# A Mamba-2 plus Conformer layer: first phase with more tiles in finer blocks, and the gate pairs of branch A kept in DRAM

## The chip, the core and the metric

The kernel runs on one core of a Trainium2 chip. A core has five engines with queues of their own: TensorE (PE, with its weight loads shown apart as PEld), VectorE (DVE), ScalarE (ACT), GpSimd (POOL) and SyncE (SP), which here only issues DMAs. Each engine carries out its instructions in the order in which the program was laid down and waits on semaphores. The metric is the time of one launch in device microseconds, the median of three runs.

## The reference

One layer over 256 latent tokens x and 256 context tokens, d = 2048, everything fp32.

```
shift, scale, gate (two sets) = split(silu(c) @ w_mod + b_mod, 6)      # the same for c_ctx
hx = rmsnorm(x) * (1 + scale) + shift                                  # 2048 channels
z, xbc, dt, glu, gates = split(hx @ w_in)                              # 4096, 6144, 128, 4096, 4096
xbc = silu(conv5(xbc)); x, B, C = split(xbc)                           # 4096, 8 x 128, 8 x 128
y = scan forwards and backwards over (x, B, C, softplus(dt)), 8 groups of 8 heads, chunks of 128;
    the latent scan starts from the context's last state
y_a = rmsnorm((y + d_skip * x) * silu(z)) @ w_proj_a
cf  = silu(layernorm(conv31(u * sigmoid(v)))) ; y_b = cf @ w_proj_b    # u, v = glu
x  += gate1 * ((sigmoid(g_a) * y_a + sigmoid(g_b) * y_b) @ w_out)
x  += gate2 * swiglu(modulate(rmsnorm(x)))
out = rmsnorm(x)
```

Context tokens only feed the scan's starting state, so of the projection they need x, B and dt (and not z, C, glu or the gates).

## The kernel before

Channels lie on the partitions and tokens on the free axis: 512 columns are 256 latent tokens followed by 256 context tokens. Each weight tile is loaded as fp32 (the name w, six buffers, 512 KB each, issued on SP), split into a rounded part wh by an ACT cast (line 113) and the rest wl by a DVE subtraction (line 114), and both are given a high scheduling priority. hx is kept as such a pair too. A unit is one weight tile of some k rows of 128 and 256 output columns. A "wide" 128-column tile gives results for all 512 tokens with three matmuls of 512 columns per k (lines 143, 144, 146); a "narrow" one serves latent tokens alone with one matmul of 512 columns and one of 256 (lines 151, 153). x, B and dt are wide; C, z, glu and the gates are narrow, and of a narrow tile the two halves of the accumulator are added by fold (lines 157 to 161: an ACT copy and a DVE addition for each of two tiles). Accumulators come from a PSUM pool named acc with four buffers, so two pairs of tiles.

**Phase one.** hx is not known at the start: its shift and scale come from w_mod (33.5 MB for these two). So the 16 k are cut into blocks, BLOCKS = (1, 1, 2, 2, 2, 4, 4) at line 32. While block q is computed, w_mod for block q+1 is fetched and multiplied by mod_units (matmuls in line 370, a small one in line 377, transposes of x in line 389). Of each block, six units are computed: dt; two pairs of x tiles each for groups 0 and 1; B and C of group 0. Each has its own accumulator, and DVE adds the block's part to a sum in SBUF (line 469; the sum of dt is dt_raw). In the last block the sum goes to a scratch tile, and conv (line 236) follows on it: an ACT pass, four DVE taps (line 246) and a Silu on ACT (line 249). After dt of the last block, dt_chain computes softplus, the cumulative sums and the weights wx.

**The scan stages.** Eight stages, one for each group: a generator ssd(stage - 1) is advanced beside a list of tasks, each of which computes one pair of tiles over all 16 k in four units. In stage 1 these are bcpair(1) (B and C of group 1), xpair(2, 0) and xpair(2, 1) (the x tiles of group 2); later stages add zpair (z, the output gate). The scan begins with transposes of B and x into PSUM, yfm (ACT, line 578), a copy btok (line 580), the weighing of x by wx (DVE, line 566) and the first matmuls with it (lines 585 and 586). gpair computes a pair of tiles of the first branch's gates g_a: one in stage 7 and four in stage 8, held in xc buffers.

**After the scan.** A stage that normalizes the Conformer branch (layernorm) is advanced beside the other eleven gate pairs, three of g_a and eight of g_b. Then come the two projections, w_out, and the FFN. A background stream computes the remaining four vectors of w_mod on DVE; a hook called once per unit advances it by 102 steps in 226 calls. At the end of each half vector it has a reduction over the partitions (matmuls in line 499, an ACT copy, transposes in line 504).

The order of instructions is made by a scheduler from the program text, with the high-priority parts moved forward by up to 450 instructions.

## Time and profile before

| | us |
|---|---|
| median of 3 runs | 2410.69 (2408.48 to 2411.11) |
| the profiled execution | 2409.69 |
| its span (first to last instruction) | 2407.9 |
| PE busy / weight loads | 2346.0 / 1976.3 |
| DVE / ACT / POOL busy | 1639.7 / 1266.5 / 131.2 |
| data moved | 509.41 MB, mean 212 GB/s |

A span is what the profiler saw from the first instruction to the last; 1.8 us of the profiled execution lie outside it. PEclk is the TensorE clock granted in a stretch, as a share of the full one. "Idle before" in a timeline's brackets is the time that the engine waited ahead of the instruction, and the arrow names what ended the wait. A tile's name stands without its number.

### The profile page before, as it was taken

To read this page: it belongs to the slowest core of one execution; us is meant where nothing else is said; L and a number is where in the kernel's file an instruction comes from. 1 tells how busy PE (TensorE), PEld (TensorE's weight loads), DVE (VectorE), ACT (ScalarE), POOL (GpSimd) and SP (SyncE) were. 2 spreads that over 40 slices of the span, in tenths; PEclk is the share of its full clock that TensorE was granted. 3 is DMA by queue.
4 is the path that set the end of the run, shared out by engine and by line. 5 is a ranking of instruction groups with operands and counts; after the bars stand their busy time and mean duration, and the time that the engine had idled before them with its cause. 6 is when DMAs were issued, how large, how long until landed. Compare 5 with 4: busy or idle time off the path is not lost.

```text
span 2407.9 us, 35235 instructions
## 1 busy us (share of the span) xinstructions
PE 2346.0 (97%) x13400; PEld 1976.3 (82%) x13400; DVE 1639.7 (68%) x2134; ACT 1266.5 (53%) x1980; POOL 131.2 (5%) x165
## 2 busy tenths in 40 slices
PE   6899999999999999999999999999999999999998
PEld 3668788888888788888888888888888888888888
DVE  4559867676676876888978676777666666655554
ACT  4335866656566675554575444446444444444443
POOL 1000000100000000010300000010000000000000
PEclk9999999999999999999999999999999999999999
DMA  9984445545455566888789887896777677766663
GB/s 280 289 280 139 134 135 153 160 125 162 136 148 155 163 199 192 266 264 282 246 267 295 261 282 251 276 288 190 219 231 223 210 230 225 222 193 193 192 192 114
DMA packets 468457, 509.41 MB, mean 212 GB/s; under 512 B 18147, under 2 KB 438194, under 8 KB 467776
## 3 DMA queue, kind: packets, MB, share of 16 engines
q1 hardware_dynamic: 461936, 488.74, 66.4%
q0 software_dynamic: 5792, 17.35, 2.2%
q8 instruction: 105, 1.72, 0.3%
q10 hardware_dynamic: 560, 1.08, 0.1%
q14 instruction: 64, 0.52, 0.1%
HBM read 496.35 MB, written 10.75 MB: 211 GB/s over the span
## 4 chain that ended last, share of the span: by engine, by line
PE 84%; DMA 7%; issue 4%; DVE 4%; ACT 2%; POOL 0%; SPq 0%; DVEq 0%; ACTq 0%; POOLq 0%
PE acc L151 38%; PE acc L153 20%; PE acc L143 6%; PE acc L144 6%; PE acc L146 6%; DMA w<-in_w_mod_dram 4%; PE acc L155 2%; DVE wl L114 2%; PE ss L667 1%; DMA cs<-cs_d 1%; PE ss L637 1%; PE tp L558 1%; PE ss L370 1%; DMA w<-in_w_in_dram 1%; DMA yst<-yg_d 1%
## 5 line engine op out<-in xcount | busy, mean ns | idle before, releaser
L114 DVE TENSOR_TENSOR wl<-w,wh 128x1024 fp32r<-128x1024 f32 (+3 forms) x702 | 847.2, 1211 | 486.0 <-ACT wh L113 484.8
L113 ACT CAST wh<-w 128x1024 fp32r<-128x1024 f32 (+3 forms) x702 | 717.0, 1023 | 703.8 <-PE acc L151 459.4
L151 PE MATMUL acc<-hx,wh 128*128 128x512 f32 x1556 | 433.0, 397 | 0.0
L151 PE MATMUL acc<-h,wh 128*128 128x512 f32 x1320 | 366.9, 397 | 4.7 <-DVE h L985 2.4
L151 PEld LDWEIGHTS acc<-hx,wh 128*128 128x128 f32 x1556 | 271.6, 189 | 40.9 <-issue 2.6
L153 PEld LDWEIGHTS acc<-hx,wl 128*128 128x128 f32 x1664 | 254.8, 188 | 35.6
L143 PE MATMUL acc<-hx,wh 128*128 128x512 f32 x656 | 265.7, 406 | 4.1 <-ACT wh L113 3.0
L153 PE MATMUL acc<-hx,wl 128*128 128x256 f32 x1664 | 264.9, 281 | 0.0
L151 PEld LDWEIGHTS acc<-h,wh 128*128 128x128 f32 x1320 | 231.5, 190 | 38.9 <-issue 4.5
L144 PE MATMUL acc<-hx,wh 128*128 128x512 f32 x656 | 259.2, 396 | 0.0
L153 PEld LDWEIGHTS acc<-h,wl 128*128 128x128 f32 x1408 | 215.9, 189 | 30.1
L493 DVE SCALAR_TENSOR_TENSOR mac<-w,silc,mac 128x1024 f32<-128x1024 f32 x120 | 154.7, 1289 | 120.2 <-DMA w<-in_w_mod_dram 119.8
L153 PE MATMUL acc<-h,wl 128*128 128x256 f32 x1408 | 223.7, 281 | 0.0
L146 PE MATMUL acc<-hx,wl 128*128 128x512 f32 x656 | 184.2, 394 | 0.0
L151 PE MATMUL acc<-hid,wh 128*128 128x512 f32 x602 | 166.3, 396 | 0.0
L143 PEld LDWEIGHTS acc<-hx,wh 128*128 128x128 f32 x656 | 123.8, 189 | 39.8 <-ACT wh L113 7.9
L146 PEld LDWEIGHTS acc<-hx,wl 128*128 128x128 f32 x656 | 123.9, 189 | 27.8 <-DVE wl L114 0.8
L144 PEld LDWEIGHTS acc<-hx,wh 128*128 128x128 f32 x656 | 124.2, 189 | 25.7 <-issue 1.6
L151 PE MATMUL acc<-yg,wh 128*128 128x512 f32 x496 | 136.6, 395 | 0.0
L151 PEld LDWEIGHTS acc<-hid,wh 128*128 128x128 f32 x602 | 103.6, 189 | 13.8
L153 PEld LDWEIGHTS acc<-hid,wl 128*128 128x128 f32 x616 | 94.4, 189 | 13.1
L618 ACT ACTIVATE cs<-cs,ncs 128x128 f32<-128x128 f32 x256 | 81.6, 390 | 32.4 <-DMA cs<-cs_d 30.6
(350 smaller groups left out, 2743.3 us busy)
## 6 DMA issues: line engine op xcount, KB each, us to landing
w<-in_w_in_dram SPq DMA_DIRECT2D x248, 512.0 KB, 4.3
w<-in_w_mod_dram SPq DMA_DIRECT2D x192, 512.0 KB, 4.9
w<-in_w_ffn_gate_dram SPq DMA_DIRECT2D x88, 512.0 KB, 4.5
w<-in_w_ffn_up_dram SPq DMA_DIRECT2D x88, 512.0 KB, 4.6
w<-in_w_ffn_down_dram SPq DMA_DIRECT2D x88, 512.0 KB, 3.5
w<-in_w_proj_a_dram SPq DMA_DIRECT2D x64, 512.0 KB, 5.2
w<-in_w_in_dram SPq DMA_DIRECT2D x74, 256.0 KB, 3.9
cs<-cs_d SPq DMA_DIRECT2D x32, 512.0 KB, 5.6
```

Of the source, the lines that this page charges most:

```text
L113: A.copy(out=hi[:, :n], in_=t[:, :n])
L114: V.tensor_tensor(out=lo[:, :n], in0=t[:, :n], in1=hi[:, :n].bitcast(F32), op=ALU.subtract)
L143: E.matmul(o, wj(hi, k), act(kofs + k)[:, 0, :ncol], start=kofs + k == kbeg, stop=False)
L144: E.matmul(o, wj(hi, k), act(kofs + k)[:, 1, :ncol], start=False, stop=False)
L146: E.matmul(o, wj(lo, k), act(kofs + k)[:, 0, :ncol], start=False, stop=last and k == nk - 1)
L151: E.matmul(o2, wj(hi, k), act(kofs + k)[:, :, :T], start=kofs + k == kbeg, stop=False)
L153: E.matmul(o[:, :T], wj(lo, k), act(kofs + k)[:, 0, :T], start=False, stop=last and not hold)
L155: E.matmul(o2, wj(hi, nk - 1), act(kofs + nk - 1)[:, :, :T], start=False, stop=True)
L370: E.matmul(b[32 * j:32 * j + 32, :fb], sil[:, rr, :], wt[:, r, :], start=rr < 4, stop=rr >= KD - 4)
L493: V.scalar_tensor_tensor(out=ac, in0=wt, scalar=silc[:, k - 1:k], in1=ac, op0=ALU.mult, op1=ALU.add)
L558: E.transpose(out=b[:, i * P:(i + 1) * P], in_=v, identity=ident)
L618: A.activation(out=t4[:, r, j], in_=t4[:, r, j], func=AF.Identity, bias=ncs[:, cc, r * 64 + hs + j:r * 64 + hs + j + 1])
```

## The change

Phase one has the blocks (1, 1, 2, 2, 2, 2, 2, 4) and takes eight units in each: B and C of group 1 and the first pair of x tiles of group 2 are added. Stage 1 of the scan therefore has neither bcpair(1) nor xpair(2, 0); it gets three gate pairs, and xpair(2, 1) after them. Stage 7 has one gate pair as before, stage 8 four, so all eight of g_a are done by the end of the scan. Each gate pair is folded into a tile named sz (one buffer) and stored by a POOL DMA to a DRAM scratch, eg_d; after the scan eight POOL DMAs load them back into ga, and sigmoid and the multiplication with the branch's 1/rms follow at the start of the normalizing stage, which now has only the eight pairs of g_b, and hands out layernorm's steps by a table. The xc pool has ten buffers instead of nine; sta and y share buffers of other tags. The hook is called 224 times rather than 236, at the same 102 in 226 (the reduction at its end has lines 503 and 508 after the change).

```diff
--- before.py
+++ after.py
@@ -29,7 +29,7 @@
 UK = 4
 UB = UK * 256
 NW32, NWH, NWL = 6, 4, 4
-BLOCKS = (1, 1, 2, 2, 2, 4, 4)
+BLOCKS = (1, 1, 2, 2, 2, 2, 2, 4)
 HP = 450
 NSTEP = 15
 
@@ -80,6 +80,7 @@
 
     xT_d = dpool.tile([P, KD, T], F32, name="xT_d")
     x1_d = dpool.tile([P, KD, T], F32, name="x1_d")
+    eg_d = dpool.tile([P, KD, T], F32, name="eg_d")
     yg_d = dpool.tile([P, 32, T], F32, name="yg_d")
     cs_d = dpool.tile([2, P, P], F32, name="cs_d")
     ec_d = dpool.tile([2, P, P], F32, name="ec_d")
@@ -225,7 +226,7 @@
     pa1 = pas.enter_context(pool("pa1", "right"))
 
     def xct():
-        return pa1.tile([P, 512], F32, tag="xc", name="xc", bufs=9)
+        return pa1.tile([P, 512], F32, tag="xc", name="xc", bufs=10)
 
     def bt():
         return pa1.tile([P, 512], F32, tag="Bt", name="Bt", bufs=2)
@@ -319,9 +320,9 @@
         V.tensor_copy(out=sel, in_=ident[:, 0:2])
         for j in range(1, 4):
             V.tensor_tensor(out=sel, in0=sel, in1=ident[:, 32 * j:32 * j + 2], op=ALU.add)
-        sta = p0.tile([P, 2 * P], F32, name="sta")
+        sta = p0.tile([P, 512], F32, tag="h32", name="h32", bufs=3)
         stb = p0.tile([P, 512], F32, tag="ev", name="ev", bufs=2)
-        st = [sta[:, :P]] + [stb[:, i * P:(i + 1) * P] for i in range(4)] + [sta[:, P:]]
+        st = [sta[:, :P]] + [stb[:, i * P:(i + 1) * P] for i in range(4)] + [sta[:, P:2 * P]]
         if vecs.n % P:
             V.memset(st[-1], 0.0)
         for vi, (ap, o, n) in enumerate(vecs.rows):
@@ -426,12 +427,15 @@
             pass
 
         dt_raw = p0.tile([P, 512], F32, name="dt_raw")
-        xts0 = [xct() for _ in range(8)]
+        xts0 = [xct() for _ in range(10)]
         Bt0, Ct0 = bt(), ct()
+        Bt1, Ct1 = bt(), ct()
         pairs = [([(OFF_XBC, P)], [dt_raw], [1]),
                  ([(OFF_Z, 256)], xts0[0:2], [1, 1]), ([(OFF_Z + 256, 256)], xts0[2:4], [1, 1]),
                  ([(OFF_B, P), (OFF_C, P)], [Bt0, Ct0], [1, 0]),
-                 ([(OFF_Z + 512, 256)], xts0[4:6], [1, 1]), ([(OFF_Z + 768, 256)], xts0[6:8], [1, 1])]
+                 ([(OFF_Z + 512, 256)], xts0[4:6], [1, 1]), ([(OFF_Z + 768, 256)], xts0[6:8], [1, 1]),
+                 ([(OFF_B + P, P), (OFF_C + P, P)], [Bt1, Ct1], [1, 0]),
+                 ([(OFF_Z + 1024, 256)], xts0[8:10], [1, 1])]
 
         sums = []
 
@@ -468,7 +472,7 @@
                         else:
                             V.tensor_tensor(out=pt if sm is None else sm, in0=pt, in1=a, op=ALU.add)
                     if sm is not None:
-                        conv(sm, 512 if wide[j] else T, {1: j, 2: 2 + j, 3: 32 + 8 * j, 4: 4 + j, 5: 6 + j}[i], pt)
+                        conv(sm, 512 if wide[j] else T, {1: j, 2: 2 + j, 3: 32 + 8 * j, 4: 4 + j, 5: 6 + j, 6: 33 + 8 * j, 7: 8 + j}[i], pt)
                 if last and i == 0:
                     dtc = dt_chain(dt_raw, p0.tile([P, D], F32, tag="xt", name="xt", bufs=4))
                     next(dtc)
@@ -669,7 +673,7 @@
                     return yo
 
                 def yadd(yo, r):
-                    t = ptile([P, 4, P], "y")
+                    t = ptile([P, 4, P], "btok")
                     V.tensor_tensor(out=t, in0=m4(yo), in1=ecb[cc][:, r], op=ALU.mult)
                     V.tensor_tensor(out=yf, in0=yf, in1=t, op=ALU.add)
                 ydp = ssb()
@@ -731,8 +735,8 @@
             bc_[g] = (B_, conv(a[1][:, :T], T, 40 + g, ct()))
 
         xt_ = {g: [] for g in range(G)}
-        xt_[0], xt_[1] = xts0[0:4], xts0[4:8]
-        bc_ = {0: (Bt0, Ct0)}
+        xt_[0], xt_[1], xt_[2] = xts0[0:4], xts0[4:8], xts0[8:10]
+        bc_ = {0: (Bt0, Ct0), 1: (Bt1, Ct1)}
         yr = {g: [] for g in range(G)}
         csb = {}
 
@@ -743,15 +747,17 @@
                 hi, lo = unit_cols(w_in, k0, UK, [(OFF_GLU + j * 256, 256)])
                 mm_unit(a, hi, lo, UK, k0, KD, [0, 0], hxa)
                 yield
-            early.append(fold(a, xct().rearrange("p (i t) -> p i t", i=2)))
+            t = fold(a, ptile([P, 2, T], "sz", 1))
+            nc.gpsimd.dma_start(out=eg_d[:, 2 * j:2 * j + 2, :], in_=t)
+            early.append(j)
         for stage in range(1, G + 1):
             zs = [(zpair(gg, j, yr[gg]), 2.56) for gg in
                   {2: [0], 3: [1], 4: [2], 5: [3], 6: [4], 7: [5], 8: [6, 7]}.get(stage, []) for j in range(2)]
-            gs_ = [(gpair(j), 2.56) for j in {7: [0], 8: [1, 2, 3, 4]}.get(stage, [])]
-            xs_ = [(xpair(stage + 1, j), 5.12) for j in range(2)] if stage + 1 < G else []
-            tasks = [(bcpair(stage), 3.84)] if stage < G else []
+            gs_ = [(gpair(j), 2.56) for j in {1: [0, 1, 2], 7: [3], 8: [4, 5, 6, 7]}.get(stage, [])]
+            xs_ = [(xpair(stage + 1, j), 5.12) for j in range(stage == 1, 2)] if stage + 1 < G else []
+            tasks = [(bcpair(stage), 3.84)] if 1 < stage < G else []
             if xs_:
-                tasks += [t for i in range(2) for t in zs[i:i + 1] + xs_[i:i + 1]]
+                tasks += gs_ + [t for i in range(2) for t in zs[i:i + 1] + xs_[i:i + 1]]
             else:
                 tasks += zs[:2] + gs_ + zs[2:]
             sg = ssd(stage - 1, xt_[stage - 1], *bc_[stage - 1], yr[stage - 1])
@@ -779,9 +785,9 @@
     ga = gbp.tile([P, KD, T], F32, name="ga")
     gb = gbp.tile([P, KD, T], F32, name="gb")
     rsta = gbp.tile([P, T], F32, name="rsta")
-    for j, t in enumerate(early):
-        A.activation(out=ga[:, 2 * j:2 * j + 2, :], in_=t, func=AF.Sigmoid)
     pas.close()
+    for j in early:
+        nc.gpsimd.dma_start(out=ga[:, 2 * j:2 * j + 2, :], in_=eg_d[:, 2 * j:2 * j + 2, :])
 
     macs = ExitStack()
     macp = macs.enter_context(pool("macp"))
@@ -871,16 +877,16 @@
                     yield
 
         ln = layernorm()
-        for j in range(16):
-            t, o = (ga, gb)[j // 8], j % 8
-            t = t[:, 2 * o:2 * o + 2, :]
-            if j >= len(early):
-                fold(pair(w_in, OFF_GLU + j * 256, KD, hxa, hook), t)
-                A.activation(out=t, in_=t, func=AF.Sigmoid)
-                if j > len(early):
-                    next(ln, None)
-            if j < 8:
-                V.tensor_tensor(out=t, in0=t, in1=rsta.unsqueeze(1).to_broadcast([P, 2, T]), op=ALU.mult)
+        for j in range(8):
+            t = ga[:, 2 * j:2 * j + 2, :]
+            A.activation(out=t, in_=t, func=AF.Sigmoid)
+            V.tensor_tensor(out=t, in0=t, in1=rsta.unsqueeze(1).to_broadcast([P, 2, T]), op=ALU.mult)
+        for j in range(8):
+            t = gb[:, 2 * j:2 * j + 2, :]
+            fold(pair(w_in, OFF_GLU + D + j * 256, KD, hxa, hook), t)
+            A.activation(out=t, in_=t, func=AF.Sigmoid)
+            for _ in range((0, 2, 2, 2, 1, 1, 1, 1)[j]):
+                next(ln, None)
         for _ in ln:
             pass
     hxs.close()
```

VectorE at the end of phase one and the start of the scan, before. xc, Bt and Ct are the conv's tiles, wl the weight rests, xw the weighed x of line 566, and sz a fold of bcpair.

```order
L246 SCALAR_TENSOR_TENSOR xc<-xt,vt,xc 128x2x254 x2
L246 SCALAR_TENSOR_TENSOR xc<-xt,vt,xc 128x2x255 x2
L114 TENSOR_TENSOR wl<-w_2547,wh 128x1024
L246 SCALAR_TENSOR_TENSOR xc<-xt,vt,xc 128x2x255 x2
L246 SCALAR_TENSOR_TENSOR xc<-xt,vt,xc 128x2x254 x2
L246 SCALAR_TENSOR_TENSOR Bt<-acc,vt,Bt 128x2x254
L566 TENSOR_TENSOR xw<-tp,wx 128x512 x2
L114 TENSOR_TENSOR wl<-w_2611,wh 128x1024
L246 SCALAR_TENSOR_TENSOR Bt<-acc,vt,Bt 128x2x255 x2
L730 TENSOR_TENSOR acc<-sz,acc 128x256
L566 TENSOR_TENSOR xw<-tp,wx 128x512 x2
```

The same place after the change (conv's taps are line 247 there, the weighing line 570, the fold's addition line 162):

```order
L247 SCALAR_TENSOR_TENSOR Ct<-xt,vt,Ct 128x254
L247 SCALAR_TENSOR_TENSOR xc<-xt,vt,xc 128x2x254 x2
L247 SCALAR_TENSOR_TENSOR xc<-xt,vt,xc 128x2x255 x4
L247 SCALAR_TENSOR_TENSOR xc<-xt,vt,xc 128x2x254 x2
L570 TENSOR_TENSOR xw<-tp,wx 128x512 x2
L162 TENSOR_TENSOR sz<-sz,acc 128x256 x2
L570 TENSOR_TENSOR xw<-tp,wx 128x512
L625 TENSOR_TENSOR cs<-cs 128x512
L570 TENSOR_TENSOR xw<-tp,wx 128x512
L162 TENSOR_TENSOR sz<-sz,acc 128x256
L570 TENSOR_TENSOR xw<-xs,wx 128x512
L162 TENSOR_TENSOR sz<-sz,acc 128x256
```

More taps stand in a row ahead of the first xw, none of B's is left for later, and the first additions of a gate pair's fold follow the first two xw.

PE around its first scan matmul before (tp are transposes, acc the accumulators of a task, ss those of the scan):

```order
L143 MATMUL acc<-hx,wh 128x512
L558 MATMUL tp<-ident,xc 128x128 x4
L144 MATMUL acc<-hx,wh 128x512
L143 MATMUL acc<-hx,wh 128x512
L144 MATMUL acc<-hx,wh 128x512
L146 MATMUL acc<-hx,wl 128x512 x2
L585 MATMUL ss<-xw,btok 128x512
L586 MATMUL ss<-xw,btok 128x512
L558 MATMUL tp<-ident,xc 128x128 x4
```

and after, where lines 152, 154 and 156 are a narrow pair's matmuls; the row of line 152 that stands alone is the first matmul of the third gate pair:

```order
L154 MATMUL acc<-hx,wl 128x256 x2
L562 MATMUL tp<-ident,Bt 128x128 x4
L154 MATMUL acc<-hx,wl 128x256 x2
L156 MATMUL acc<-hx,wh 128x512
L562 MATMUL tp<-ident,xc 128x128 x8
L152 MATMUL acc<-hx,wh 128x512
L589 MATMUL ss<-xw,btok 128x512
L590 MATMUL ss<-xw,btok 128x512
L562 MATMUL tp<-ident,xc 128x128 x4
L596 MATMUL ss<-xw,btok 128x512
L597 MATMUL ss<-xw,btok 128x512
```

The projection's wide matmuls have gone from this place, and a gate pair's start stands between the transposes and the scan's first matmuls.

ACT at the same place after the change (line 161 is the fold's copy):

```order
L250 ACT_TABLE_LOAD
L250 ACTIVATE xc<-xc 128x512 x4
L250 ACTIVATE Bt<-Bt 128x512
L250 ACTIVATE Ct<-Ct 128x256
L250 ACTIVATE xc<-xc 128x512 x2
L582 ACTIVATE yfm<-xc,dcol 128x256 x4
L161 COPY sz<-acc 128x256 x2
L584 COPY btok<-tp 128x512
L582 ACTIVATE yfm<-xc,dcol 128x256
L622 ACTIVATE cs<-cs,ncs 128x128 x9
L161 COPY sz<-acc 128x256 x2
```

The first fold's copies stand behind the Silu of eight tiles and four yfm.

## Rows read from the trace of the kernel before

**Rows 1.** The page, busy us (share of the span) and instructions of each engine.
```profile
PE 2346.0 (97%) x13400; PEld 1976.3 (82%) x13400; DVE 1639.7 (68%) x2134; ACT 1266.5 (53%) x1980; POOL 131.2 (5%) x165
```

**Rows 2.** Windows: us, length, busy us (PE, PEld, DVE, ACT, POOL), PEclk, DMA share, GB/s.
```profile
20.00:100.00 80.00, 74.44 (x559) 49.90 (x557) 46.71 (x101) 30.82 (x71) 3.30 (x6) 0.98 0.93 279
100.00:180.00 80.00, 70.57 (x497) 48.91 (x496) 40.90 (x74) 25.60 (x48) 4.43 (x8) 0.94 0.91 285
180.00:260.00 80.00, 80.00 (x387) 65.47 (x386) 74.42 (x113) 43.77 (x63) 2.55 (x4) 1.00 0.48 136
260.00:300.00 40.00, 38.24 (x198) 29.11 (x197) 34.24 (x49) 36.17 (x79) 4.15 (x4) 1.00 0.52 142
```

**Rows 3.** Timeline (start, us, instruction, idle before), DVE, dt_raw, blocks 2 to 7.
```profile
47.11 0.69 DVE L469 TENSOR_TENSOR dt_raw<-dt_raw,acc 128x512 f32<-128x512 f32 x1 [0.74 <-PE acc L146]
...
66.55 0.69 DVE L469 TENSOR_TENSOR dt_raw<-dt_raw,acc 128x512 f32<-128x512 f32 x1 [1.27 <-PE acc L146]
...
85.78 0.69 DVE L469 TENSOR_TENSOR dt_raw<-dt_raw,acc 128x512 f32<-128x512 f32 x1 [0.87 <-PE acc L146]
...
107.67 0.69 DVE L469 TENSOR_TENSOR dt_raw<-dt_raw,acc 128x512 f32<-128x512 f32 x1 [0.88 <-PE acc L146]
...
146.66 0.69 DVE L469 TENSOR_TENSOR dt_raw<-dt_raw,acc 128x512 f32<-128x512 f32 x1 [2.92 <-PE acc L146]
...
190.36 0.69 DVE L469 TENSOR_TENSOR dt_raw<-dt_raw,acc 128x512 f32<-128x512 f32 x1 [0.90 <-PE acc L146]
```

**Rows 4.** Timeline, DVE, the end of phase one.
```profile
226.07 1.23 DVE L114 TENSOR_TENSOR wl<-w,wh 128x1024 fp32r<-128x1024 f32 x1
227.21 1.40 DVE L246 SCALAR_TENSOR_TENSOR xc<-xt,vt,xc 128x508 f32<-128x508 f32 x2
...
236.90 0.48 DVE L246 SCALAR_TENSOR_TENSOR Ct<-xt,vt,Ct 128x254 f32<-128x254 f32 x1
...
250.31 2.72 DVE L246 SCALAR_TENSOR_TENSOR xc<-xt,vt,xc 128x510 f32<-128x510 f32 x4
...
253.60 1.28 DVE L566 TENSOR_TENSOR xw<-tp,wx 128x512 f32<-128x512 f32 x2
```

**Rows 5.** Timeline, PE, the first scan matmul.
```profile
256.79 1.11 PE L585 MATMUL ss<-xw,btok 128*128 128x512 f32 x2
```

**Rows 6.** Timeline, PE, phase one.
```profile
104.11 1.93 PE L370 MATMUL ss<-w,sil 128*32 128x256 f32 x32
105.98 0.50 PE L143 MATMUL acc<-hx,wh 128*128 128x512 f32 x1
...
151.29 0.61 PE L377 MATMUL tp<-sel,ev 128*128 128x2 f32 x4 [0.49 <-ACT ev L374]
...
152.76 0.50 PE L143 MATMUL acc<-hx,wh 128*128 128x512 f32 x1
...
187.44 0.39 PE L143 MATMUL acc<-hx,wh 128*128 128x512 f32 x1
...
190.16 0.39 PE L143 MATMUL acc<-hx,wh 128*128 128x512 f32 x1
```

**Rows 7.** Timeline, PE, narrow tiles of four k.
```profile
1653.83 1.09 PE L151 MATMUL acc<-h,wh 128*128 128x512 f32 x4
...
1655.24 1.09 PE L151 MATMUL acc<-h,wh 128*128 128x512 f32 x4
```

**Rows 8.** Timeline, ACT, the first scan stage.
```profile
252.41 1.29 ACT L249 ACTIVATE xc<-xc 128x512 f32<-128x512 f32 x2 [3.42 <-DVE xc L246]
...
254.55 1.70 ACT L578 ACTIVATE yfm<-xc,dcol 128x256 f32<-128x256 f32 x4
...
256.62 0.36 ACT L729 COPY sz<-acc 128x256 f32<-128x256 f32 x1
```

**Rows 9.** Windows of 10 us in phase one and ahead of the last gate stage.
```profile
110.00:120.00 10.00, 6.31 (x32) 4.37 (x33) 2.02 (x5) 2.55 (x6) 0.54 (x1) 0.59 1.07 344
...
980.00:990.00 10.00, 10.00 (x59) 8.73 (x58) 9.94 (x17) 5.68 (x8) 0.00 (x0) 1.00 1.03 350
```

## The prediction

> **What bounds the kernel now.** I read the busy line of the page first. PE is busy 97% of the span, but its weight loads only 82% [rows 1]. The Trainium skill ("Perfetto Trace Analysis", Identifying the Most-Contended Engine) calls matmul busy time a poor measure and weight-load busy time a good one; the rows bear it out, since by weight loads the first phase stands out.
>
> Then the windows. From 20 to 180 us PE loads weights for 49.9 and 48.9 of 80 us while the DMA engines are 0.93 and 0.91 busy; from 180 on it loads for 65.5 of 80 and DMA drops to 0.48 [rows 2]. So phase one is limited by transfers and PE about equally, and from 180 on PE has no idle time (80.00 of 80) while DVE, at 74.4 of 80, is close behind. From 260 to 300 PE is idle 1.8 of 40.
>
> The third view is VectorE's order in time. Its six evictions of dt_raw, the first result of each block, are a clock for phase one: 47.11, 66.55, 85.78, 107.67, 146.66, 190.36 [rows 3], so intervals of 19.4, 19.2, 21.9, 39.0 and 43.7.
>
> The last view is the end of phase one: the first weighing of x (line 566) stands at 253.60 on DVE, right behind the last conv taps [rows 4], and the first scan matmul at 256.79 on PE [rows 5], 63.2 and 66.4 after the last dt eviction. PE hardly waits there, because it still has units to run.
>
> **A, the start of the last block.** PE's price of one 128-column tile, wide (three matmuls per k): 190.16 - 187.44 = 2.72 for four k, so 0.68 per k; narrow (two per k): 1655.24 - 1653.83 = 1.41, so 0.35 per k [rows 6, 7]. Four w_mod tiles take 105.98 - 104.11 = 1.87, so 0.47 each; four small records of line 377 with two k of transposes take 152.76 - 151.29 = 1.47 [rows 6].
> Before, a two-k block has 10 wide tiles and one narrow: 2 x (10 x 0.68 + 0.35) = 14.3. Eight w_mod tiles add 3.8, lines 377 and 389 add 0.5 + 1.5 = 2.0: 20 in all, and the trace has 19.2 and 21.9. After, it has 13 wide and two narrow: 2 x (13 x 0.68 + 0.70) = 19.1, with the rest 24.8, say 25. Its bytes rise from 5.6 to 6.2 MB (eight w_mod tiles of 0.52 MB, 256 rows of 1408 or 1920 columns): at 285 GB/s [rows 2] 21.6 us. So PE is the limit, and the free time that was there is less than the work put in.
> The first two blocks have one k and grow by 1.5 and 0.6 (a k of the three new tiles is 2.4, of which DMA waits hide some). Four two-k blocks follow, 4 x 25, and then one that computes two k while it fetches w_mod for four. Before, that was 9.8 MB in 39.0; now it is 10.4 MB, 39.5 (buffers already ahead take the rest), with 19.1 + 11.4 = 30.5 as PE's floor. Sum 139.5 + 2.1, against 19.2 + 21.9 + 39.0 + 43.7 = 123.8: **+18**. Low end +8 (the long block at PE's floor), high end +26 (each of the five a further 1.6 for transfers, as 21.9 stands over 20).
>
> **B, from there to PE's next free buffer.** DVE carries out its rows in order, and PE runs ahead only as far as its accumulators reach. After the change DVE has ahead of its first weighing: 8 taps for the two new x tiles and 4 for B, less one B tap that before stood there, 11 x 0.68 = 7.5 (250.31: four in 2.72); 4 C taps at up to 0.48 = 1.9; three wide sums at 0.69 and two narrow ones at about 0.4, 2.9; and 16 weight subtractions against 12, 4 x 1.14 = 4.6 [rows 3, 4]. That is 16.9: the first weighing moves from 63.2 to 80 after the dt eviction.
> PE does not have work until then. Its remaining units of the last block are at most 12 x 2.72 + 2 x 1.41 = 35.4, two gate pairs are 2 x 8 x 1.41 = 22.6, transposes some 2: 60 [rows 6, 7]. The third gate pair needs accumulators, and these come free by the fold of the first. The fold's ACT copy stands behind the last Silu (1.29 for two), four yfm (1.70) and its own two copies (0.36 each) [rows 8]; its DVE add stands behind all taps and two weighings (1.28) [rows 4]. So PE takes up work at about 82 where before it had its first scan matmul at 66.4: **+16**, bounds +10 (the scheduler's taps overlap idle that DVE had: 5.6 of 80 in that window [rows 2]) and +20.
>
> **C, work already done at that point.** Two gate pairs, 22.6, which before ran later. Of the pairs that moved into phase one, B/C of group 1 had already run before this point too, and x of group 2 all but some 3 us. **-25.5**. This is sure, since the total of matmuls is unchanged.
>
> **D, the clock.** A gap of some 20 us in PE's work is new. The one stretch with repeated waits on transfers, 110 to 120, shows a granted clock of 0.59, and the wider windows 0.94 to 1.00 [rows 2, 9]. At 0.59 for 10 us up to 4.1 is lost; I take **+2** (0 to 4.1).
> **E.** Before's own idle between 260 and 300, 1.8 [rows 2], goes into the same gap: **-2**.
> **F.** The background stream of w_mod is called 224 times rather than 236, and its last reduction (lines 503 and 508) lands right ahead of the second RMSNorm. PE has four small matmuls, an ACT copy and two transposes there with nothing beside them: 0.5 + 0.36 + 0.3 by like rows [rows 6, 8]: **+1** (0 to 1.5).
> **G, the gates through DRAM.** Eight stores and eight loads of 256 KB, on POOL's queue, 5% busy [rows 1]. Weights are issued on SP's queue and not behind them. The loads, 2.1 MB, come while the window 980 to 990 already moves 350 GB/s [rows 9], and the sigmoids that use them have the first pair of the last stage as cover. **0**; if the weights wait for them in full, 2.1 / 0.35 = 6. The normalization steps have eight pairs to lie beside rather than eleven, but are handed out one or two per pair: 0.
>
> Sum: 18 + 16 - 25.5 + 2 - 2 + 1 = +9.5 on the profiled 2409.7: 2419.2. The median of the runs is 1.0 above the profiled run, so **2420**.
>
> **Rivals.**
> *Faster: the gate pairs fill the gap.* Place: the first scan stage. If PE may go on to the third gate pair as soon as the second ends, about 58 to 60 after the dt eviction, B is 24 smaller and D is 0: 9.5 - 24 - 2 = -16.5, so 2394. For it: three gate pairs need neither conv nor scan, and phase one's weight loads leave 30 of 80 us [rows 2]. The price is decided by one row: whether the first fold's add stands ahead of the conv taps on DVE. It stands behind them in the order shown, and DVE was busy 74.4 of 80 before any of it was added. The Trainium skill ("Perfetto Trace Analysis", Optimization Strategy) says that kernels whose most contended engine changes with time may gain by interleaving those regimes, which is what this rival would be; this trace shows the two regimes [rows 2], and whether PE has a free buffer in the second is not in that rule.
> *No change: phase one takes the work nearly free.* A at its low end of 8 gives -0.5: 2410. For it: weight loads idle more than a third of phase one. Against: the sum of PE's pitches, 20, already equals the block intervals.
> *Slower still: the reload of the gates stalls the weight stream* at 960 to 1010, +6: 2426. For it: 1.03 of DMA share [rows 9]; against: PE has no wait in that same window.
>
> **How the numbers follow.** Forecast .55, faster rival .17, no change .18, slower rival .10. A measurement of this kernel tells 0.2%, 4.8 us, from no change. The forecast lies 9.5 above, and its own range, 2412 to 2428, is mostly slower (.52, with .03 for the same); the no-change case gives .15 to the same and .03 to faster; the slower rival is all slower. Together faster .20, same .18, slower .62. The range reaches down to 2400, leaving most of the faster rival out, and up to 2432 (A at its high end with some of G).
>
> **What would show it.** dt evictions near 49, 69, 94, 119, 144, 169 and 208. One gap of 20 to 25 us on PE between 268 and 292 that ends with DVE's add of line 162, a lower granted clock right behind it. From the second scan stage on the same pitch as before, some 9 later. It is wrong if the blocks stay near 21 us (A small), or if PE is without a gap there (B small).

## The result, and the profile after

The changed kernel takes 2440.45 us (median of 4 runs, 2439.2 to 2446.35) against 2410.9 before: a ratio of 1.013, with a 95% interval of 1.0111 to 1.0148. It is slower, as forecast, but by 30 us and not by 10, and outside the range, which ended at 2432. The profiled execution has a span of 2437.5 us, 29.6 more than before.

The busy line of the page hardly moved [rows 1]; what is lost is a share of one per cent:

```profile
PE 2351.5 (96%) x13400; PEld 1980.2 (81%) x13400; DVE 1665.7 (68%) x2195; ACT 1265.5 (52%) x2000; POOL 142.8 (6%) x181
```

The windows, which answer to [rows 2] and go on to 340:

```profile
20.00:100.00 80.00, 72.32 (x539) 50.04 (x535) 47.85 (x104) 32.91 (x77) 3.27 (x6) 1.00 0.86 262
100.00:180.00 80.00, 80.00 (x531) 57.83 (x530) 54.19 (x104) 26.30 (x54) 3.25 (x6) 1.00 0.81 253
180.00:260.00 80.00, 77.50 (x422) 61.59 (x415) 69.68 (x107) 42.44 (x62) 2.17 (x4) 0.99 0.68 200
260.00:300.00 40.00, 19.70 (x105) 15.18 (x105) 33.06 (x57) 16.34 (x26) 2.02 (x3) 0.72 0.36 99
300.00:340.00 40.00, 34.45 (x171) 26.25 (x169) 24.58 (x35) 28.34 (x70) 5.61 (x6) 0.91 0.51 139
```

Phase one did take its new work: from 100 to 180 PE is never idle (70.57 of 80 before) and loads weights for 57.8 us instead of 48.9. From 260 to 300 PE works 19.7 of 40 us, while DVE works 33.1. The clock, which stood at 1.00 there before, is 0.72 in the mean.

The evictions of dt_raw on DVE, which answer to [rows 3] (five of the seven stand here; two are at 72.44 and 95.77):

```profile
49.16 0.69 DVE L473 TENSOR_TENSOR dt_raw<-dt_raw,acc 128x512 f32<-128x512 f32 x1 [1.05 <-PE acc L147]
...
121.68 0.69 DVE L473 TENSOR_TENSOR dt_raw<-dt_raw,acc 128x512 f32<-128x512 f32 x1 [1.01 <-PE acc L147]
...
147.59 0.69 DVE L473 TENSOR_TENSOR dt_raw<-dt_raw,acc 128x512 f32<-128x512 f32 x1 [1.79 <-PE acc L147]
...
173.92 0.69 DVE L473 TENSOR_TENSOR dt_raw<-dt_raw,acc 128x512 f32<-128x512 f32 x1 [2.33 <-PE acc L147]
...
212.43 0.69 DVE L473 TENSOR_TENSOR dt_raw<-dt_raw,acc 128x512 f32<-128x512 f32 x1 [1.52 <-PE acc L147]
```

A two-k block takes 25.9 us (the first of them 23.3), and the last block starts at 212.43, 22.1 later than before. At its end VectorE's first weighing, 80.7 after that eviction, stands right behind the last eight conv taps:

```profile
287.67 5.36 DVE L247 SCALAR_TENSOR_TENSOR xc<-xt,vt,xc 128x508 f32<-128x508 f32 x8
293.12 1.29 DVE L570 TENSOR_TENSOR xw<-tp,wx 128x512 f32<-128x512 f32 x2
```

Then PE's idle times around the start of the scan, from its timeline:

```profile
277.51 0.66 PE L562 MATMUL tp<-ident,xc 128*128 128x128 f32 x4 [3.43 <-DVE ncs L304]
...
294.55 1.08 PE L562 MATMUL tp<-ident,xc 128*128 128x128 f32 x4 [16.39 <-DVE xw L570]
...
296.11 0.80 PE L152 MATMUL acc<-hx,wh 128*128 128x512 f32 x1 [0.48 <-DVE sz L162]
...
303.84 1.12 PE L597 MATMUL ss<-xw,btok 128*128 128x512 f32 x2 [2.68 <-DVE xw L570]
...
332.31 1.16 PE L671 MATMUL ss<-Ct,h 128*128 128x128 f32 x8 [2.29 <-DVE yfm L685]
...
349.94 1.16 PE L671 MATMUL ss<-Ct,hb 128*128 128x128 f32 x8 [1.43 <-DVE yfm L685]
```

The gap of 3.4 + 16.4 us is the one forecast. What follows it was not: a third wait of 2.7, two of 2.3 and 1.4 much later, and matmuls at the lower clock behind all of these but the last, as the windows show (0.50 is the lower of the two levels, 1.2 GHz; PE did nothing for 10 us there). Behind the wait at 349.94 the clock stayed at 1.00.

```profile
280.00:290.00 10.00, 0.00 (x0) 0.00 (x0) 10.00 (x18) 2.20 (x4) 0.00 (x0) 0.50 0.00 0
290.00:300.00 10.00, 4.97 (x12) 2.66 (x13) 5.76 (x10) 4.27 (x10) 0.56 (x1) 0.54 0.48 104
300.00:310.00 10.00, 6.73 (x26) 4.61 (x25) 5.55 (x10) 8.22 (x20) 1.60 (x2) 0.83 0.36 107
330.00:340.00 10.00, 7.71 (x37) 6.06 (x36) 7.21 (x11) 6.04 (x16) 1.35 (x1) 0.83 0.54 138
```

Where the 29.6 us arise is read at landmarks that both kernels pass. One is the first scan matmul of each stage (line 585, now 589): the answer on that line gives the start of its first and its last instance, in stages 1 and 8. Before:

```profile
L585 PE MATMUL ss<-xw,btok x16: 592/592/677, 256.8 to 864.2; 128*128 128x512 f32 x16
```

and after (the three numbers are the shortest, median and longest in ns):

```profile
L589 PE MATMUL ss<-xw,btok x16: 592/592/1061, 296.7 to 921.1; 128*128 128x512 f32 x16
```

At stage 8 the changed kernel is 56.9 us later and has three gate pairs done that the other has not, 3 x 8 x 1.41 = 33.8 [rows 7]: 23.1 us are lost. At stage 2 it is 23.3 by the same count, so all of it is lost before stage 2, and nothing from there to stage 8. Its first scan matmul before, and after:

```profile
311.85 1.02 PE L585 MATMUL ss<-xw,btok 128*128 128x512 f32 x2
...
368.98 1.02 PE L589 MATMUL ss<-xw,btok 128*128 128x512 f32 x2
```

The two later landmarks are the first matmul of the Conformer's projection, which waits for the normalization, and the first of the FFN, before

```profile
1267.20 1.64 PE L151 MATMUL acc<-cfx,wh 128*128 128x512 f32 x6 [2.79 <-DVE cfx L896]
...
1643.30 4.60 PE L151 MATMUL acc<-h,wh 128*128 128x512 f32 x10 [2.44 <-DVE h L985]
```

and after:

```profile
1296.33 2.90 PE L152 MATMUL acc<-cfx,wh 128*128 128x512 f32 x6 [5.40 <-DVE cfx L902]
...
1675.36 3.90 PE L152 MATMUL acc<-h,wh 128*128 128x512 f32 x10 [2.35 <-DVE h L991]
```

So 29.1 us are lost by the one and 32.1 by the other; 2.5 come back in the FFN.

### The profile page after: what moved, and what is told of

Same layout as the page of the kernel before. It is cut to its first block, busy times and chain, and to the rows that moved or that the text cites. A ratio compares the mean times of both kernels' runs of the same rounds, so it can differ in the third digit from the quotient of the medians.

```text
span 2437.5 us, 35438 instructions
## 1 busy us (share of the span) xinstructions
PE 2351.5 (96%) x13400; PEld 1980.2 (81%) x13400; DVE 1665.7 (68%) x2195; ACT 1265.5 (52%) x2000; POOL 142.8 (6%) x181
## 4 chain that ended last, share of the span: by engine, by line
PE 88%; DMA 5%; DVE 3%; ACT 1%; issue 1%; POOL 1%; SPq 0%; ACTq 0%; DVEq 0%; POOLq 0%
PE acc L152 39%; PE acc L154 21%; PE acc L144 7%; PE acc L147 6%; PE acc L145 6%; DMA w<-in_w_mod_dram 3%; PE acc L156 2%; PE ss L671 1%; PE ss L371 1%; DVE wl L115 1%; POOL var L864 1%; DMA cs<-cs_d 1%; PE ss L641 1%; PE tp L562 1%; DMA w<-in_w_in_dram 1%
```

## The experiments

Theory 1 at the start: VectorE's backlog of conv taps makes the gap, and the loss behind the gap is its consequence. Theory 2: that loss belongs to the scan stage's list of tasks. Theory 3: PE waits for accumulators or something else. "Lost at stage 8" is worked out as above, from the last start on the line of the first scan matmul: last start - 864.2 - 33.8. It is read from one trace of each kernel, and carries what that trace lost in phase one: in the change, e1, e2, e5, e6, e8 and e9 phase one up to its last block is laid out by the same lines, and the last dt eviction stands at 212.43, 215.27, 217.64, 216.86, 215.29, 215.60 and 218.22. So differences of a few us at the landmarks need not come of the edit.

**e1, taps left out** (so x of groups 1 and 2 and B/C of group 1 are not what they should be, in part):

```diff
-conv(sm, ..., pt)
+conv(sm, ..., pt, (0, 1, 3, 4) if i < 4 else ())   # no DVE taps for units 4 to 7
```

> The changed kernel, with the conv taps of the last four units of phase one left out (x of group 1 in the second pair and of its first, B/C of group 1, x of group 2): 28 wide taps and 4 narrow ones, some 28 x 0.68 + 4 x 0.4 = 21 us of VectorE ahead of the first weighing. Theory 1 (VectorE's backlog makes the gap on PE, and the loss behind the gap, between 296 and 360, is its consequence): the first weighing stands 60 to 62 us after the last dt eviction instead of 80.7, PE's idle time of 16.4 + 3.4 goes down to under 4, and the loss behind it goes too: 2440 - 20 - 10 = 2410 (2406 to 2415). Theory 2 (the loss behind the gap comes from the shorter task list of the first scan stage, whatever the gap): the gap goes, the loss stays: 2420 to 2424. Theory 3 (PE waits for accumulators or for something else than the taps): 2435 or more.

Measured: 2426.77 us, ratio 1.0065 (1.0048 to 1.0081). PE around the scan's start:

```profile
279.44 1.09 PE L562 MATMUL tp<-ident,xc 128*128 128x128 f32 x4 [4.38 <-DVE xw L570]
...
292.95 1.12 PE L651 MATMUL ss<-xw,btok 128*128 128x512 f32 x2 [1.44 <-DVE xw L570]
...
314.17 1.16 PE L671 MATMUL ss<-Ct,h 128*128 128x128 f32 x8 [2.57 <-DVE yfm L685]
```

The first weighing comes 62.7 us after the last dt eviction (278.01 - 215.27) instead of 80.7, and the gap falls from 16.4 to 4.4: VectorE's backlog is its cause, and theory 3 falls. Lost at stage 8: 903.4 - 898.0 = 5.4. But the wait at 314 stands as before (2.57 where it was 2.29), so theory 1 does not hold for all of the loss behind the gap. The total is 17 above theory 1's 2410, and above theory 2's range too: the losses after the scan are there as well, 18.5 by the FFN (1661.80 - 1643.30).

**e2, the x pair ahead of the gate pairs in stage 1:**

```diff
-tasks += gs_ + [t for i in range(2) for t in zs[i:i + 1] + xs_[i:i + 1]]
+tasks += [t for i in range(2) for t in zs[i:i + 1] + xs_[i:i + 1]] + gs_
```

> The changed kernel with the x pair ahead of the three gate pairs in the first scan stage. With four accumulators PE can run two pairs before it needs VectorE. Theory 1 (backlog and two pairs): these two are now 21.8 + 11.3 = 33.1 us instead of 22.6, VectorE's rows up to the first weighing are the same, so the gap is 10.5 shorter and the loss behind it a little smaller: 2428 (2422 to 2431). Rival (the gap's length is set by what PE has queued behind the first scan matmuls, not by the work ahead of it): no change, 2437 to 2443.

Measured: 2425.33 us, 1.0053 (1.0034 to 1.0072). The gap:

```profile
298.73 1.09 PE L562 MATMUL tp<-ident,xc 128*128 128x128 f32 x4 [11.76 <-DVE xw L570]
```

It is 11.76 instead of 16.39 + 3.43, and of the two waits on line 671 0.26 and 0.43 are left, so more came back than the gap. Lost at stage 8: 907.9 - 898.0 = 9.9.

**e3, the gates' half alone** (phase one as before, the three gate pairs between the two x pairs):

```diff
-BLOCKS = (1, 1, 2, 2, 2, 2, 2, 4)
+BLOCKS = (1, 1, 2, 2, 2, 4, 4)          # six units, bcpair(1) and both xpair(2, j) back in stage 1
-tasks += gs_ + [t for ...]
+tasks += [t for i in range(2) for t in zs[i:i + 1] + xs_[i:i + 1] + (gs_ if i == 0 else [])]
```

> Phase one as before the change (six units, the old blocks, B/C of group 1 and both x pairs of group 2 in the first scan stage), with the other half of the change alone: the three gate pairs in the first scan stage between the two x pairs, all eight through DRAM, eight pairs in the normalizing stage. Theory 1 (the cost of the change lies in phase one's end, this half only adds what was lost later: some 3 in the normalizing stage and 3 to 4 ahead of the second RMSNorm): no gap at the start of the scan, 2411 + 6 = 2417 (2412 to 2420). Rival (the gate pairs in the first scan stage are the cost, by their folds on ACT and VectorE and by the DRAM round trip): 2428 or more, with a gap in the first scan stage.

Measured: 2416.86 us, 1.0025 (1.0015 to 1.0035), as theory 1 has it. There is no gap, and nothing is lost at stage 8 (896.4 - 898.0 = -1.6), but 3.7 at the Conformer's projection and 5.8 at the FFN:

```profile
1270.94 2.90 PE L152 MATMUL acc<-cfx,wh 128*128 128x512 f32 x6 [4.12 <-DVE cfx L899]
...
1649.13 4.63 PE L152 MATMUL acc<-h,wh 128*128 128x512 f32 x10 [2.35 <-DVE h L988]
```

So the two halves of the change cost about 23 and 6.

**e4, seven units** (x of group 2 not in phase one, both x pairs first in stage 1):

```diff
-xts0 = [xct() for _ in range(10)]
+xts0 = [xct() for _ in range(8)]        # no unit for OFF_Z + 1024; xpair(2, 0), xpair(2, 1), then gpair 0 to 2
```

> The changed kernel without the x pair of group 2 in phase one (seven units, nine xc buffers), both x pairs of group 2 first in the first scan stage and the three gate pairs behind them. Theory 1: a two-k block is 2 x (11 x 0.68 + 0.70) + 5.7 = 22 on PE, about what the transfers take, so phase one still fills its free time; VectorE has 8 taps and two sums fewer (6.8) ahead of the first weighing, 74 after the dt eviction, and PE has 26 + 43.5 + 3 = 72 of work until then: gap 0 to 5. Relative to the changed kernel 20 to 30 less, to the one before -10 + 6: 2400 to 2415. Rival (finer blocks and the new units cost more in phase one than they fill): 2420 or more without a gap.

Measured: 2422.23 us, 1.0055 (1.0036 to 1.0074). The gap is gone, but two-k blocks take 23.1 (120.32 to 143.43) and PE later waits 5.06 us for an accumulator that a conv still reads. The expectation of a gain over the kernel before was wrong: 14.2 us later at the last block for 12 x (0.68 + 0.35) = 12.4 us of work moved is no gain in phase one. The rival of this run, that the new units cost more in phase one than they fill, has its condition met: over 2420 and no gap.

**e5, the gate pairs' weight subtractions on GpSimd:**

```diff
-hi, lo = unit_cols(w_in, k0, UK, [(OFF_GLU + j * 256, 256)])
+hi, lo = unit_cols(w_in, k0, UK, [(OFF_GLU + j * 256, 256)], G_ if j < 3 else None)
```

> The changed kernel with the weight subtractions of the three gate pairs of the first scan stage on GpSimd instead of VectorE (12 instructions; eight of them stood ahead of the first weighing). Nothing is left out. Theory 1 (VectorE's backlog sets the gap): 8 x 1.14 = 9.1 us less on VectorE, so the first weighing stands 71 to 72 us after the last dt eviction instead of 80.7, PE's gap is 9 shorter, and the lost time of the restart a little smaller: 2430 (2426 to 2433). The waits on the scan's loads of cs between 325 and 350 stay. Rival (GpSimd's subtractions, whose 1.3 us for 512 columns make 2.7 us for 1024, are as slow as the narrow units that need them, so PE waits for them instead): 2438 to 2450.

Measured: 2448.78 us, 1.0169 (1.015 to 1.0188), slower than the change. By the expectation's count VectorE lost nine us of work, and the first weighing still came 84.1 after the dt eviction. Its taps, seven in a row, took 11.10 us where seven at 0.68 make 4.8 [rows 4]:

```profile
280.27 11.10 DVE L247 SCALAR_TENSOR_TENSOR xc<-xt,vt,xc 128x508 f32<-128x508 f32 x7
```

GpSimd's subtractions beside these taps kept about their usual length (2.74 in the median, here 5.67 for two). The last one, which starts behind the slowed taps, took four times that, and VectorE's taps beside it were at their usual 0.73:

```profile
283.17 5.67 POOL L115 TENSOR_TENSOR wl<-w,wh 128x1024 fp32r<-128x1024 f32 x2 [0.57 <-ACT wh L114]
293.05 10.03 POOL L115 TENSOR_TENSOR wl<-w,wh 128x1024 fp32r<-128x1024 f32 x1 [4.20 <-ACT wh L114]
```

The time lies in the range of the rival (2438 to 2450), but its mechanism is not seen: of PE's waits over 1 us between 200 and 420 all seven end with VectorE, none with a subtraction on GpSimd.

**e6, the background stream faster:**

```diff
-hook = bg(mgen, 102, 226)
+hook = bg(mgen, 102, 212)
```

> The changed kernel with the background stream of w_mod at 102 steps in 212 calls instead of 102 in 226, so that its last reduction ends some ten units earlier. Theory 1 (of the late losses, the reduction ahead of the second RMSNorm and the waits for wl around it at the end of w_out are the ones from 1620 to 1700, about 5 us): 2436 (2434 to 2438). Rival (these waits come of VectorE's load by the output conversions there, not of the stream): no change, 2439 to 2442.

Measured: 2445.99 us, 1.0151 (1.0136 to 1.0166): no gain. From the Conformer's projection to the FFN it takes 4.6 us less than the change (1676.79 - 1302.37 = 374.4 against 379.0), but the projection itself waits 10.19 us for the normalization instead of 5.40. The stream's steps are VectorE work; that they were only taken from one place and put in another fits these two numbers, and is not shown beyond them.

**e7 and e11, the finer blocks alone on the kernel before:**

```diff
-BLOCKS = (1, 1, 2, 2, 2, 4, 4)
+BLOCKS = (1, 1, 2, 2, 2, 2, 2, 4)
```

> The kernel before with the finer blocks alone, (1, 1, 2, 2, 2, 2, 2, 4) with its six units. Theory 1 (the sum of PE's pitches and of the transfers sets phase one, not the cut): two blocks of 39.0 and 43.7 become two of about 21 and one of 39, so the last dt eviction moves by -2 to +1, no gap: 2410 (2407 to 2413). Rival (finer blocks leave PE less to do beside the transfers): 2416 or more.

> The kernel before with the finer blocks alone, again with more rounds: its trace showed 4 us less in phase one, its time no difference. If that trace was typical, a ratio of 0.998 with an interval under 1; if not, 1.000.

Measured: 2407.95, 0.9996 (0.9985 to 1.0007), and in e11, the same kernel, 2405.9, 0.9981 (0.9972 to 0.9991). The last block starts at 188.85 in e7 and at 191.09 in e11, against 190.36. The cut is not what costs; by e11 it gains 5 us, by e7 nothing that can be told from no change.

**e8, e2 and e5 and e6 together:** no edit of its own.

> The changed kernel with the three edits together: x pair first in the first scan stage, the gate pairs' weight subtractions on GpSimd, the stream at 102 in 212. Theory 1 (they add up): the gap of 11.8 that the x pair first leaves shrinks by 4 x 1.14 to 9.1, so to 3 to 7; the restart's loss goes with it; 4 us at the end: 2425 - 7 - 3 - 4 = 2411 (2407 to 2417). Rival (the gap is filled, but the time comes back in the scan stage, whose own chain of loads is then the limit): 2418 to 2424.

Measured: 2436.78, 1.0108 (1.0091 to 1.0125). That is 11 slower than e2 alone and above both expectations. The gap is 13.92 instead of e2's 11.76, and VectorE's taps take up to 2.89 us, as in e5.

**e9, a fourth gate pair in stage 1:**

```diff
-{1: [0, 1, 2], 7: [3], 8: [4, 5, 6, 7]}
+{1: [0, 1, 2, 3], 8: [4, 5, 6, 7]}
```

> The changed kernel with a fourth gate pair in the first scan stage (and none in the seventh). The question is the loss behind the gap. Theory 2 (after the gap the scan's loads of cs, 5 to 9 us each, lie bare, as the list of the first stage is too short to hide them: ACT waits 12.9 us for them and its casts stand behind): 11.3 us more of units between the scan's steps, so the two waits of PE on the scan's sums (2.29 and 1.43) go and the loss between 300 and 360 is some 5 smaller; the gap stays at 16; the seventh stage may give a part back: 2436 (2433 to 2440). Theory 1 (that loss is a consequence of the gap): it stays at 12: 2438 to 2443, or more by what the seventh stage loses.

Measured: 2445.49, 1.0146 (1.0127 to 1.0164). One of the two late waits is gone, the other is 3.54 instead of 1.43, and 25.9 are lost at stage 8 (923.9 - 898.0). Counted from the last dt eviction, which came 5.8 later than in the change's trace, that is 3.0 less than in the change; but e6, which alters nothing in the scan, has 2.6 less by the same count. So theory 2, in the form that the list is too short, is not borne out.

**e10, the DRAM trip alone** (the kernel before, its five early gate pairs stored and loaded again):

```diff
-early.append(fold(a, xct().rearrange("p (i t) -> p i t", i=2)))
+t = fold(a, ptile([P, 2, T], "sz", 1)); nc.gpsimd.dma_start(out=eg_d[...], in_=t); early.append(j)
```

> The kernel before with one thing alone: its five early gate pairs go through DRAM (one in stage 7, four in stage 8, folded into sz, stored, and loaded again after the scan) instead of waiting in xc buffers; eleven pairs stay in the normalizing stage. The question is the 6 us that the gates' half of the change cost with phase one as before. Theory A (the cost is the shorter normalizing stage, eight pairs beside the same VectorE work, and the denser w_out): nothing here: 2409 to 2412. Theory B (the cost is the way through DRAM and the single sz buffer): 2413 to 2417.

Measured: 2409.84, 1.0001 (0.999 to 1.0012). The trip, of five pairs here and eight in the change, costs nothing that can be told from no change.

**e12 and e13, a last block of six k,** with the gate pairs first, and with the x pair first:

```diff
-BLOCKS = (1, 1, 2, 2, 2, 2, 2, 4)
+BLOCKS = (1, 1, 2, 2, 4, 6)             # the six k of a unit loaded as four and two
```

> The changed kernel with phase one cut as (1, 1, 2, 2, 4, 6) and nothing else (a unit of six k is loaded as four and two). VectorE's rows behind the last dt eviction are the same 80 us plus one weight subtraction per unit, but PE has half as much again to do in the last block: about 12 x 4.1 + 2 x 2.1 = 53 us instead of 35, and with two gate pairs and the small ones 79. Theory 1 (the gap is the difference between VectorE's backlog and PE's work, and the loss behind it is its consequence): the gap shrinks from 20 to 0 to 8 and the loss behind it with it, the blocks before keep PE busy as they did: 2440 - 15 - 6 = 2419 (2412 to 2424). Theory 2 (the loss behind the gap belongs to the scan stage that follows units with their conv still running): the gap goes, 8 to 12 stay: 2424 to 2430. Rival (a block of four k that fetches w_mod for six waits for transfers, 16.5 MB at 285 GB/s or 58 us against PE's 55, and loses more than the gap): 2435 or more.

> The same with the x pair ahead of the gate pairs in the first scan stage, which gives PE 10.6 us more to do before it needs an accumulator back: 90 us of work against some 82 on VectorE. Theory 1: no gap, and no loss behind it: 2425 (the x pair first with the old cut) - 12 - 6 = 2407 (2402 to 2413), faster than the kernel before only if the losses after the scan, some 7, are made good by phase one. Theory 2: 2412 to 2419.

Measured: e12 2429.4, 1.0083 (1.0062 to 1.0104); e13 2415.35, 1.0023 (1.0013 to 1.0033). The gap in e12 and the late waits:

```profile
285.90 1.09 PE L564 MATMUL tp<-ident,xc 128*128 128x128 f32 x4 [5.79 <-DVE xw L572]
...
323.12 1.87 PE L673 MATMUL ss<-Ct,h 128*128 128x128 f32 x8 [3.11 <-DVE yfm L687]
...
340.69 1.16 PE L673 MATMUL ss<-Ct,hb 128*128 128x128 f32 x8 [1.34 <-DVE yfm L687]
```

And the windows of e13 over the same stretch, where no wait of PE is longer than 1.23 us:

```profile
260.00:300.00 40.00, 38.47 (x186) 29.99 (x185) 34.83 (x50) 26.92 (x50) 1.80 (x1) 1.00 0.50 131
300.00:340.00 40.00, 38.71 (x242) 32.71 (x241) 31.59 (x43) 31.14 (x73) 5.51 (x6) 1.00 0.85 225
```

With nearly the same VectorE work ahead of the scan (the first weighing 85.2 after the last dt eviction) and more of PE's beside it, the gap shrinks to 5.8, and with the x pair first it is gone, together with everything behind it: lost at stage 8 are 13.5 in e12 (911.5 - 898.0) and -3.6 in e13 (894.4 - 898.0). The time of e12 lies in the range of theory 2, not of theory 1. The late pair of waits on line 671 or 673 is there in every kernel with the gate pairs first (the change, e1, e5, e6, e12; one of them in e9), with a gap of 4.4 us as with one of 16.4, and all but absent in e2, behind a gap of 11.8, and in e13.

**e14 and e15, e13 with the normalizing stage's pairs given back:**

```diff
-{1: [0, 1, 2], 7: [3], 8: [4, 5, 6, 7]}
+{1: [0, 1, 2], 7: [3], 8: [4]}          # e15: 8: [4, 5]; the other pairs of g_a in the normalizing stage
```

> The kernel with the cut (1, 1, 2, 2, 4, 6) and the x pair first, but with five gate pairs of g_a in the scan (three in stage 1, one in 7, one in 8) and three in the normalizing stage, which has eleven pairs again as before the change. Theory A (the 8 to 10 us lost after the scan come of the normalizing stage's shorter list): that loss goes, and the last scan stage, with one gate pair where it had four, loses 0 to 8 for want of cover: 2407 to 2413. Theory B (they come of something else that the gates' half brought, such as the reload): 2414 or more, with the losses between 1020 and 1300 still there.

> The same with one more gate pair in stage 8 and ten pairs in the normalizing stage. Theory A: between the two, most of the late loss gone and less lost in stage 8: 2407 to 2412. Theory B: 2414 or more.

Measured: e14 2411.45, 1.001 (0.9996 to 1.0025); e15 2406.36, 0.9986 (0.9974 to 0.9998). Both times fit theory A, e15 lying just below its range. The projection and the FFN in e13, then in e14, then in e15:

```profile
1269.33 2.90 PE L152 MATMUL acc<-cfx,wh 128*128 128x512 f32 x6 [5.16 <-DVE cfx L904]
...
1650.58 4.63 PE L152 MATMUL acc<-h,wh 128*128 128x512 f32 x10 [2.35 <-DVE h L993]
```

```profile
1265.30 2.90 PE L152 MATMUL acc<-cfx,wh 128*128 128x512 f32 x6 [2.77 <-DVE cfx L904]
...
1644.25 4.60 PE L152 MATMUL acc<-h,wh 128*128 128x512 f32 x10 [2.44 <-DVE h L993]
```

```profile
1269.40 1.65 PE L152 MATMUL acc<-cfx,wh 128*128 128x512 f32 x6 [3.83 <-DVE cfx L904]
...
1642.17 4.48 PE L152 MATMUL acc<-h,wh 128*128 128x512 f32 x10 [2.35 <-DVE h L993]
```

PE's wait at the projection is shorter with the pairs given back. But the last block starts at 197.92, 193.57 and 197.52 in these three traces, with the same lines up to there, and counted from it the projection follows after 1071.4, 1071.7 and 1071.9: up to there nothing is won, and the last scan stage, with fewer gate pairs, has a new wait (2.24 in e14, 1.28 in e15). From the projection to the FFN it is 381.3, 379.0 and 372.8, against 376.1 before. So the late loss goes with the way in which the pairs are dealt out; that it arises in the normalizing stage alone is not shown. e15 and the finer blocks alone (e11) are the two versions whose interval lies below the kernel before, with ratios 0.14% and 0.19% under it.

## Why the forecast was wrong

| step | forecast | measured |
|---|---|---|
| A, start of the last block | +18 | +22.1 (212.43 - 190.36) |
| B, from there to the first scan matmul | +16 | +17.9 (84.3 - 66.4) |
| C, work already done | -25.5 | -26.0 (79 matmuls of 512 columns and 64 of 256 more) |
| D and E, up to stage 2 | 0 | +9.3 (the rest to 23.3) |
| G, up to the Conformer's projection | 0 | +5.8 (29.1 - 23.3) |
| F, up to the FFN | +1 | +3.0 (32.1 - 29.1) |
| FFN | 0 | -2.5 |
| sum | +9.5 | +29.6 |

**A** had the right limit: from 100 to 180 PE was never idle, and a two-k block's 24.8 us was 25.9 (the first 23.3). Of the 4 us that it was short 3.3 are in the second block, 23.3 instead of 20.0; in e1, e2, e5, e6, e8 and e9 that block takes 24.7 to 26.3. The new tiles' growth there was put at 0.6, with transfers hiding the rest of their 2.4; it was 3.8 and more, and why it is more than the 2.4 stays open.

**B** held in its parts: the first weighing, worked out at 80 us after the dt eviction, came at 80.7. The step named the wrong release. PE went on when the weighing had freed a transposes' buffer (the row at 294.55), not when the fold had freed accumulators (the row at 296.11, 0.48); both stand behind the same taps, so the time was nearly the same (82.1 after the dt eviction, forecast 82), and that much of the hit is luck. e1 and e12 show the cause from both sides, less work on VectorE and more on PE.

**C** can be counted: before its first scan matmul PE ran 721 matmuls of 512 columns and 96 of 256 into the accumulators, against 642 and 32 before the change. By the prediction's prices (0.227 and 0.126 us) that is 26.0 more.

**D and E** failed, and this is the step that put the forecast's mechanism out of size: "A gap of some 20 us in PE's work is new ... I take +2", less 2 for idle time that would go into the gap. The stretch between the first scan matmuls of stages 1 and 2, before and then after:

```profile
256.79:311.85 55.06, 53.30 (x271) 41.03 (x271) 47.02 (x66) 49.15 (x106) 4.15 (x4) 1.00 0.55 147
```

```profile
296.70:368.98 72.28, 65.30 (x320) 50.53 (x320) 42.59 (x58) 42.98 (x100) 6.17 (x7) 0.94 0.53 142
```

Behind the gap PE is idle 6.98 us where it was 1.76 (E had this fall to nothing), and its granted clock is 0.94 in the mean, so some 4.3 of 72.28 us are lost to it (D had 2): together the 9.3, nearly. In single rows, the scan waits again for the next weighing (2.68), its first matmuls run at the lower clock (up to 1061 ns against a median of 592), and later come the two waits on the scan's sums, the first of which takes the clock down once more.

Only a part of this tail is the gap's. Counted by matmuls as for C, it is 9.3 in the change, 8.8 in e12 with a gap of 5.8 and 5.1 in e1 with one of 4.4, all with the gate pairs first; with the x pair first it is 4.0 in e2 behind a gap of 11.8, and 0.5 in e13 without one. So some 3.5 (4.0 - 0.5) can be put down to a gap, and the rest goes with the order of the list, gate pairs or x pair first. The chain of the wait at 332.31, on ACT after the change:

```profile
328.19 1.28 ACT L622 ACTIVATE cs<-cs,ncs 128x128 f32<-128x128 f32 x4 [4.27 <-DMA cs<-cs_d]
329.38 1.03 ACT L114 CAST wh<-w 128x1024 fp32r<-128x1024 f32 x1
```

and on DVE:

```profile
330.44 1.23 DVE L115 TENSOR_TENSOR wl<-w,wh 128x1024 fp32r<-128x1024 f32 x1 [6.08 <-ACT wh L114]
331.58 0.68 DVE L685 TENSOR_TENSOR yfm<-yfm,ss 128x512 f32<-128x512 f32 x1
```

ACT waits for a load of cs, the cast for the x pair's next weights stands behind it on ACT, the subtraction waits for the cast, and the addition that frees the scan's sum stands behind the subtraction. Why PE has to wait so with one order and not with the other is not settled: ACT's waits for cs add up to 12.9 us after the change, 12.6 in e1 and 5.6 in e2 (all between 230 and 365), but to 11.7 in e3, where no wait of PE reaches 1 us.

**F and G** failed too. The term G asked whether the reload would stall the weights, and it does not (e10). It put the eight pairs of the normalizing stage in place of eleven at 0, "handed out one or two per pair", and that is the term that was wrong: e3 has this loss without the new phase one, 5.3 us from stage 8 to the projection, and e14 and e15 are faster than e13 with pairs given back. The number of pairs and the table that hands out layernorm's steps changed together, and which stage the loss is to be put down to stays open, as said there. F's +1 came out as +3.0, which no run takes apart; a faster stream (e6) wins 4.6 behind the projection and waits 4.8 longer at it.

The rival that ended faster, a gap filled by gate pairs, failed on the row it named: the fold stands behind the taps on DVE. The rival of no change (A at its low end) failed as A came out above its mean. The rival "slower still" had nearly the right size for the stretch up to the projection (6 against 5.8), by luck: PE's two longest waits there are at 1043.8 (2.35) and 1296.3 (5.40) and not at 960 to 1010, and the trip through DRAM shows no cost (e10).

The Trainium skill's advice ("Perfetto Trace Analysis", Optimization Strategy) to interleave the regimes describes what this change did to PE's stretch from 100 to 180. The trace agrees so far, 80.00 of 80 us against 70.57, and the kernel was slower all the same; e13 shows what was missing, that the engine behind, VectorE, takes part in the same count.

## What to carry to other kernels

Work moved into a phase where PE waits for transfers brings its conversions, sums and convolutions along, and these fall due when the phase ends: count the next engine's backlog at that seam against what PE can do before it needs a buffer back, and size the last block so that PE's side is the longer one (four k and 35 us failed here, six k and the longer task first did not). A gap on PE cost more than its length here, some 4 us behind 11.8 of waiting (e2), by the clock and by waits in the stage that starts behind it; the order of the tasks in that stage cost as much again. Where a stage hands out side work by tasks, taking tasks from it can be a cost of its own (e3), and giving them back takes cover from the stage that had them (e14).

## What the runs showed of the hardware

GpSimd and VectorE held each other up, one at a time. With subtractions of 128x1024 on GpSimd, VectorE's tap took up to 2.88 us against 0.74 in the median, and a subtraction of GpSimd up to 10.03 against 2.74 (e5). The long taps stand beside subtractions of about the usual length, and the long subtraction beside an unbroken row of taps of 0.73. The Trainium skill ("GPSIMD Engine Reference", Specifications) states that GpSimd shares its SBUF interfaces with VectorE, and that VectorE's instructions with two SBUF inputs contend with it. VectorE's taps have two here, and the trace agrees: the first weighing came 84.1 us after the dt eviction with the subtractions on GpSimd, and 80.7 without.
